# Three of four groups of W2 in seven block products with tokens down the partitions, and the branch weights' two parts made by transfers

## The chip, the cores and the metric

The kernel runs on one core of one Trainium2 chip. The time is the device time of one launch in microseconds (us); of several runs the median is given. TensorE (PE; PEld is its weight load), VectorE (DVE), ScalarE (ACT), GpSimd (POOL) and SyncE (SP, which only issues transfers) each have an instruction queue of their own that runs in order. Before, all transfers are issued from SP; the change issues some from POOL, which round to another type or add to what stands at the destination.

## The reference, cut to what matters

Two layers of an encoder on 512 tokens of 1024 channels. Each layer has a mixing half (projections, two kinds of softmax attention, a retention, three gated branches, an output projection) and an MLP. The change lies in the MLP's second matrix and in how the branch weights are prepared.

```python
projected = jnp.einsum('bsnw,nwd->bsnd', branches, w_branch[l])
gates = jax.nn.sigmoid(gate_logits.reshape(B, S, N_BRANCHES, D))
merged = jnp.sum(gates * projected, axis=2)
h = h + jnp.einsum('bsd,de->bse', merged, w_out[l])

m = jnp.einsum('bsd,df->bsf', rms_norm(h, mlp_norm[l]), w_mlp_in[l])     # W1: 1024 -> 4096
m = jnp.square(jax.nn.relu(m))
h = h + jnp.einsum('bsf,fd->bsd', m, w_mlp_out[l])                       # W2: 4096 -> 1024
```

## The kernel before, in words

All arithmetic is float32. The matmuls run on the type `F32R`; for it the kernel cuts every operand into a first part `hi` (ScalarE's copy rounds it) and a rest `lo` (VectorE subtracts), and each product is three matmuls: hi x hi, hi x lo, lo x hi (`passes`, line 568). Weights come in pieces ("quarters") of [128, 1024], 512 KB each: SP loads one into `stage`, ScalarE makes `w_hi`, VectorE makes `w_lo` (`cut_to`, line 512). The pool of such parts, `p_w`, holds six pairs.

Activations stand with channels down the partitions and tokens along the columns. W1 (`pair`, line 644) goes by pairs of 128 output columns in Winograd's form of Strassen's scheme: seven block products instead of eight, each of 12 matmuls with 256 columns, 84 in all. Its weights are cut by `cut_pair` (line 535), which takes three pairs of `p_w` (and one half pair of `p_wh`). The products run in the order 1, 2, 6, 5, 7, 4, 3; the first pair of parts serves 1 and 2, the second 6 and 5, the third 7 and 3.

W2 goes in four groups of 1024 hidden channels (`mlp`, line 1335). A group has eight units of 128 output channels; a unit is one sum in PSUM over eight tiles of hidden channels, three matmuls each with 512 columns: 24 matmuls (`prod_a`). The first group's sums are copied to SBUF (`mo`), the second and third are added to them, the third is multiplied by 1 / rms (`mo<-mo,rs`) and added to the stream `h`, the fourth goes from PSUM to `h`. `mlp_order` (line 52) weaves the four pairs of the next group's W1 into a group's W2: two within it, two behind it.

The merge at the end of the mixing half computes for each of three branches eight gate units and eight `proj` units; a branch has four quarters of weights (`("br", n, i)`), 12 a layer.

Every instruction is first noted and then put in an order (`Plan.order`, line 303): a simulated run in which each engine takes its first ready instruction, by the place where it was noted, with estimated durations (`price`, line 212) and the pools' free slots. The emitted program has that fixed order on each engine's queue, so an instruction whose input is late holds up what stands behind it.

Of the kernel before, what the change touches and what calls it, by code (L numbers as in the profile page):

```python
# [28 lines left out]
# positions of the small per-layer vectors in the row that every partition receives  # L29
# [14 lines left out]
GATE_PAIRS = {1: 8, 0: 2, 2: 0}  # L44
GATE_BANKS = ("mm", "sc", "tr")
# the gates after which the right operands of those pairs are made, four steps in all
TURN_AT = [(1, 4), (1, 6), (1, 6), (0, 0)]
# after which units of W2 the first pairs of the next group's W1 come
WOVEN = (3, 6)


def mlp_order():
    """W1 goes by pairs of units, W2 by units, in four groups of eight; a group's W1 starts within the W2 before it."""
    pairs = lambda g, k: [("w1", g, 2 * i) for i in k if g < 4]
    seq = pairs(0, range(4))
    for g in range(4):
        n = 0
        for i in range(8):
            while n < len(WOVEN) and WOVEN[n] == i:
                seq += pairs(g + 1, [n])  # L60
                n += 1
            seq.append(("w2", g, i))
        seq += pairs(g + 1, range(n, 4))
    return seq


def weight_plan():
    """Quarters of [128, 1024] in the order in which the core uses them: (key, matrix, rows, columns)."""
# [40 lines left out]
    for what, g, i in mlp_order():  # L109
        if what == "w1":  # L110
            for f in (g * 8 + i, g * 8 + i + 1):
                a_unit(("w1", f), "w_mlp_in", cols(f * 128, 128))
        else:
            a_unit(("w2", g, i), "w_mlp_out", cols(i * 128, 128), r0=g * 1024)
    return plan
# [5 lines left out]
# units whose weights are used two by two, in seven products instead of eight (Winograd's form of Strassen's)  # L121
PAIRED = {WIDX["w1", f] for f in range(0, 32, 2)} | {WIDX["gate", n, i] for n in GATE_PAIRS for i in range(GATE_PAIRS[n], 8, 2)}

BUFS_STAGE = 2
BUFS_W = 6
BUFS_WH = 2
BUFS_MID = 3
AHEAD_LOAD = 6
AHEAD_SPLIT = 2
# [27 lines left out]

class Ref:
    """A view of such a tile."""
# [82 lines left out]
class Op:  # L242
    __slots__ = ("engine", "name", "args", "kwargs", "key", "cost", "deps", "tiles", "new", "left", "outs", "end",
                 "ready")


class Plan:
    """Notes instructions as nc's engines are called, and issues them in the order of a simulated run."""
# [15 lines left out]
    def note(self, engine, name, args, kwargs):  # L264
# [30 lines left out]
        o.cost = price(engine, name, kwargs) if engine != "sync" else self.dma_price(kwargs)  # L295
        self.ops.append(o)
# [6 lines left out]
    def order(self):  # L303
        """A run in which every engine takes the first of its ready instructions, by key."""
# [7 lines left out]
        # slots: tiles of a tag in the order of their keys  # L312
# [11 lines left out]
        def ahead(g, pos):  # L324
            """Tiles before this one that have no slot yet."""
# [21 lines left out]
        while len(result) < n:  # L347
# [22 lines left out]
            for e in self.ENGINES:  # L370
# [27 lines left out]
                heapq.heappush(events, (now + o.cost + self.LATENCY.get(e, 0.0), 0, pick))  # L398
# [29 lines left out]
class Core:  # L428
    def __init__(self, ctx, tc, a):
# [3 lines left out]
        def pool(name, bufs, **k):  # L433
            return Pool(ctx.enter_context(tc.tile_pool(name=name, bufs=bufs, **k)), bufs, "space" in k)
# [6 lines left out]
        self.p_s = pool("s", 1)  # L441
# [17 lines left out]
        self.loaded = self.cut = 0  # L459
        self.stage, self.w = {}, {}  # L460
# [20 lines left out]
    # ---- weights: load and cut into two parts that TensorE's fast float32 takes exactly  # L481
    def load(self, n):
        while self.loaded < min(n, L * NQ):
            q = self.loaded
            t = self.p_stage.tile([128, 1024], F32, tag="stage", name="stage")
            self.nc.sync.dma_start(out=t, in_=self.a["w"][q])
            self.stage[q] = t
            self.loaded += 1

    def prefetch(self, i):  # L490
        n = min(i + AHEAD_SPLIT, L * NQ)
        while self.cut < n:
            self.load(self.cut + BUFS_STAGE)
            self.cut_to(self.cut + 1)
        self.load(min(i + AHEAD_LOAD, self.cut + BUFS_STAGE))

    def first_quarter(self, x):
        """The first quarter comes in pieces of 512 columns, each behind the tile of the stream that it meets."""
# [11 lines left out]
        self.loaded = self.cut = 1  # L510

    def cut_to(self, n):
        nc = self.nc
        while self.cut < n:
            q = self.cut
            if q % NQ in PAIRED:
                self.load(q + 2)
                self.w[q] = self.cut_pair(self.stage.pop(q), self.stage.pop(q + 1))
                self.cut += 2
                continue  # L520
            t = self.stage.pop(q)
            hi = self.p_w.tile([128, 1024], F32R, tag="hi", name="w_hi")
            lo = self.p_w.tile([128, 1024], F32R, tag="lo", name="w_lo")
            nc.scalar.copy(out=hi, in_=t)
            nc.vector.tensor_tensor(out=lo, in0=t, in1=hi, op=ALU.subtract)
            self.w[q] = (hi, lo)
            self.cut += 1

    def part(self, pool, n, t):
        hi = pool.tile([128, n], F32R, tag="hi", name="w_hi")  # L530
        lo = pool.tile([128, n], F32R, tag="lo", name="w_lo")
# [3 lines left out]
    def cut_pair(self, q0, q1):  # L535
        """Both parts of the seven left operands, each [128, 4 x 128]; q0 is [A11 | A12], q1 [A21 | A22]."""
        nc = self.nc
        lt, rt = slice(0, 512), slice(512, 1024)
# [15 lines left out]
    def weights(self, l, key):  # L554
        q = l * NQ + WIDX[key]
        self.prefetch(q + 1)
        return self.w[q]
# [18 lines left out]
    def head_rstd(self, ss, t, name):  # L576
        """1 / rms over a head of 64, for sums of squares that lack the token's own factor: its eps carries it."""
# [9 lines left out]
    # ---- RMSNorm: the products run on x g, and the tokens' 1 / rms scales what comes out of them  # L587
# [4 lines left out]
    def feed(self, x, k, which, u):  # L592
        """One [128 d, 512] tile of the stream: both parts of x g."""
# [4 lines left out]
    def feed_pair(self, x, j, which, u):  # L598
        """Tiles j and 4 + j of x g as right operands of the seven products: token halves B11, B12 and B21, B22."""
# [26 lines left out]
    def right(self, u, n, p, j):  # L626
        """Part p of the right operand of product n, k tile j: [128, 256 tok]."""
# [919 lines left out]
```

## Time and profile before

| what | value |
|---|---|
| median of 3 runs | 1793.13 us (1792.23 to 1793.45) |
| profiled execution, first to last instruction (span) | 1791.8 us |
| matmuls on TensorE | 10216 |
| TensorE clock granted | full in nearly every slice (1.00) |
| busy: PE, DVE, ACT, POOL | 99%, 77%, 55%, 17% of the span |
| moved by transfers | 172.50 MB, mean 96 GB/s |

The runs lie 0.4 to 1.7 us above the span of the profiled execution: that much lies around the first and last instruction. The first layer's stages in the profiled execution are: attention and projections to about 245 us, merge 245 to 517.6, output projection to 561.2, MLP to 898; the second layer repeats them.

### The profile page before, as it was taken

How to read it: one execution, taken by the hardware profiler on the slowest of the kernel's cores; microseconds unless marked ns; L12 is line 12 of the kernel's file. 1: busy time of each engine (PE TensorE's matmuls, PEld its weight loads, DVE VectorE, ACT ScalarE, POOL GpSimd, SP SyncE). 2: the span in 40 equal slices, each digit the busy share in tenths (PEclk: the TensorE clock that was granted, in tenths of full speed). 3: DMA queues.
4: the chain of work that ended last, by engine and by line, in shares of the span. 5: the costliest groups of instructions: out<-in, count | busy, mean ns of one | idle time of the engine just before them, and what ended most of it. 6: DMA issues, size and time to landing. Idle time of an engine off the chain costs nothing.

```text
span 1791.8 us, 26264 instructions
## 1 busy us (share of the span) xinstructions
PE 1767.7 (99%) x10216; PEld 1544.8 (86%) x10216; DVE 1376.4 (77%) x2084; ACT 983.2 (55%) x1568; POOL 297.1 (17%) x294
## 2 busy tenths in 40 slices
PE   8999999999999999999999999999999999999999
PEld 6887888889989989999888778888888899989897
DVE  7866797899979766678656677968999797566783
ACT  5545666784446655445444455768844466444450
POOL 3334472002210000000013335700111100000000
PEclk9999999999999999999999999999999999999999
DMA  6311212112352323333432121121133423234331
GB/s 203 105 61 49 93 49 79 59 37 95 107 170 101 118 94 118 123 115 116 152 106 71 48 80 62 59 63 56 39 104 130 159 83 134 95 102 128 121 113 56
DMA packets 53691, 172.50 MB, mean 96 GB/s; under 512 B 6336, under 2 KB 6848, under 8 KB 53568
## 3 DMA queue, kind: packets, MB, share of 16 engines
q1 hardware_dynamic: 53568, 170.84, 29.4%
q8 instruction: 80, 1.31, 0.3%
q14 instruction: 43, 0.35, 0.1%
HBM read 162.43 MB, written 8.39 MB: 95 GB/s over the span
## 4 chain that ended last, share of the span: by engine, by line
PE 82%; DVE 8%; issue 3%; POOL 3%; ACT 2%; DMA 1%; SPq 0%; DVEq 0%; ACTq 0%; POOLq 0%
PE x L411 21%; PE w L411 20%; PE gate L411 6%; PE proj L411 5%; PE wo L411 5%; PE c L411 4%; PE wtr L413 2%; PE rv L411 2%; DVE w_lo L417 2%; PE rg L411 2%; PE rq L411 2%; PE dsc L411 2%; PE gav L411 2%; PE gsc L411 2%; DVE c L417 1%
## 5 line engine op out<-in xcount | busy, mean ns | idle before, releaser
L417 ACT CAST w_hi<-stage 128x1024 fp32r<-128x1024 f32 (+1 forms) x283 | 276.6, 982 | 319.7 <-PE w L411 120.7
L417 DVE TENSOR_TENSOR w_lo<-stage,w_hi 128x1024 fp32r<-128x1024 f32 (+1 forms) x283 | 336.9, 1192 | 78.7 <-ACT w_hi L417 75.8
L411 PE MATMUL x<-u,w_hi 128*128 128x256 f32 x1472 | 273.5, 284 | 5.3 <-DVE c L417 5.3
L411 PEld LDWEIGHTS x<-u,w_hi 128*128 128x128 f32 x1472 | 232.3, 192 | 10.9 <-DVE c L417 8.2
L411 PE MATMUL x<-u,w_lo 128*128 128x256 f32 x736 | 208.0, 283 | 0.0
L411 PE MATMUL w<-ml,w_hi 128*128 128x512 f32 (+1 forms) x520 | 200.3, 386 | 0.0
L411 PE MATMUL w<-mh,w_lo 128*128 128x512 f32 (+1 forms) x520 | 200.1, 386 | 0.0
L411 PE MATMUL w<-mh,w_hi 128*128 128x512 f32 (+1 forms) x520 | 200.1, 387 | 0.0
L411 PEld LDWEIGHTS x<-u,w_lo 128*128 128x128 f32 x736 | 141.1, 192 | 0.0
L417 ACT ACTIVATE c<-c 128x512 f32<-128x512 f32 x156 | 98.4, 631 | 32.9 <-DVE c L417 30.2
L411 PEld LDWEIGHTS w<-mh,w_lo 128*128 128x128 f32 x520 | 97.8, 188 | 19.5
L411 PEld LDWEIGHTS w<-ml,w_hi 128*128 128x128 f32 x520 | 97.8, 188 | 18.7
L411 PEld LDWEIGHTS w<-mh,w_hi 128*128 128x128 f32 x520 | 97.8, 188 | 18.5
L411 PE MATMUL gate<-u,w_hi 128*128 128x512 f32 x320 | 107.3, 399 | 0.0
L411 PE MATMUL x<-t23h,w_lo 128*128 128x256 f32 x368 | 104.2, 283 | 0.0
L411 PE MATMUL x<-t23l,w_hi 128*128 128x256 f32 x368 | 104.0, 283 | 0.0
L411 PE MATMUL x<-t23h,w_hi 128*128 128x256 f32 x368 | 103.9, 283 | 0.0
L417 ACT CAST w_hi<-sa 128x1024 fp32r<-128x1024 f32 x46 | 48.5, 1053 | 77.0 <-DVE sa L417 55.9
L411 PE MATMUL c<-w_hi,u 128*128 128x512 f32 x256 | 86.1, 394 | 0.0
L417 POOL TENSOR_TENSOR gth<-gth,c 128x512 f32<-128x512 f32 x28 | 45.9, 1647 | 179.0 <-DVE c L417 179.0
L417 DVE TENSOR_TENSOR c<-x,pu 128x512 f32<-128x512 f32 x92 | 63.1, 686 | 12.0 <-PE x L411 11.3
L411 PEld LDWEIGHTS x<-t23l,w_hi 128*128 128x128 f32 x368 | 70.6, 192 | 0.0
(278 smaller groups left out, 4554.5 us busy)
## 6 DMA issues: line engine op xcount, KB each, us to landing
stage<-in_w SPq DMA_DIRECT2D x283, 512.0 KB, 3.6
h<-in_x SPq DMA_DIRECT2D x16, 256.0 KB, 5.3
mid<-h SPq DMA_DIRECT2D x16, 256.0 KB, 2.0
h<-mid SPq DMA_DIRECT2D x16, 256.0 KB, 4.8
keep<-h SPq DMA_DIRECT2D x8, 256.0 KB, 4.1
h<-keep SPq DMA_DIRECT2D x8, 256.0 KB, 3.9
out<-h SPq DMA_DIRECT2D x7, 256.0 KB, 2.0
t_ret<-in_t_ret SPq DMA_DIRECT2D x4, 256.0 KB, 4.9
```

The source lines that it names most:

```text
L411: self.nc.tensor.matmul(k.pop("out"), **k)
L413: self.nc.tensor.transpose(k["out"], k["in_"], k["identity"])
L417: getattr(getattr(self.nc, o.engine), o.name)(**k)
```

## The change

Three things are changed.

**W2's groups 0, 1 and 2** take the seven products too, with blocks of 512 hidden channels, 256 tokens and 512 output channels. The activations are now the operand that TensorE loads and the weights the one that moves, so sums come out with tokens down the partitions. A product is 2 sums of 12 matmuls with 512 columns (`wide_product`): 24 as in a unit, but seven a group. `rights` makes the seven blocks of the activations out of the group's eight tiles `c` and cuts each in parts (`xh`, `xl`). `cut_wide` makes the seven blocks of the weights: A11, A12 and A22 by `cut_dma`, the four combined ones on VectorE out of extra loads, the first of them (A21 + A22) by a transfer that adds. ScalarE copies every sum to `wp`; the first group's are stored in DRAM (`sums`), the next two groups' are added there by transfers from POOL. In group 3, which keeps its eight units, `gather` reads the 14 sums back, combines them, transposes them on TensorE (`turn`), multiplies them by 1 / rms and adds them to the stream.

**The branch weights**: `cut_dma` takes the place of `cut_to`'s cut. POOL issues a transfer that rounds DRAM's values to `hi`, ScalarE writes -hi to `lo`, POOL issues a transfer that adds the same DRAM values to `lo`. The VectorE subtraction goes; both weights are read twice.

**Pools and the planner**: `p_w` has five pairs instead of six, `sa` three buffers instead of one; weights are prepared two steps of a list `STEPS` ahead; `price` counts a matmul 11 ns longer, and POOL's transfers have estimates of their own.

```diff
-WOVEN = (3, 6)
+WIDE_GROUPS = (0, 1, 2)
+WOVEN = {True: (2, 4), False: (3, 6)}
...
+WIDE = ("A11", "A12", "A22", "S1", "S2", "S4", "S3")
+WIDE_PRODUCTS = (1, 2, 4, 5, 6, 3, 7)
...
-BUFS_W = 6
+BUFS_W = 5
-AHEAD_LOAD = 6
-AHEAD_SPLIT = 2
+AHEAD = 2
...
-            return 2.5 + n / 2.4 * (1 if n >= 256 else 4)
+            return 13.7 + n / 2.4 * (1 if n >= 256 else 4)
...
-        self.p_s = pool("s", 1)
+        self.p_s = pool("s", {"sa": 3, "sb": 1})
...
+    def cut_dma(self, q):
+        nc = self.nc
+        hi, lo = self.parts(self.p_w, 1024)
+        nc.gpsimd.dma_start(out=hi, in_=self.a["w"][q])
+        nc.scalar.activation(out=lo, in_=hi, func=AF.Copy, scale=-1.0)
+        nc.gpsimd.dma_start(out=lo, in_=self.a["w"][q], accum_op=ALU.add)
+        return hi, lo
...
+        def add(t, x):
+            nc.vector.tensor_tensor(out=t, in0=t, in1=self.load(at(x)), op=ALU.add)
+        if op == "A11":
+            w[k] = self.load(at("A21"), self.p_s, "sa")
+            nc.gpsimd.dma_start(out=w[k], in_=self.a["w"][at("A22")], accum_op=ALU.add)
+        if op[0] == "A":
+            return self.cut_dma(at(op))
+        if op == "S3":
+            w[k] = self.load(at("A21"))
+        if op != "S1":
+            add(w[k], {"S2": "A11", "S3": "A11", "S4": "A12"}[op])
+        return self.part(self.p_w, 1024, w[k])
...
-            if g == 0:
-                total[i] = self.g("mo")
-                nc.scalar.copy(out=total[i], in_=p)
-            elif g < 3:
-                nc.vector.tensor_tensor(out=total[i], in0=total[i], in1=p, op=ALU.add)
-                if g == 2:
-                    nc.vector.tensor_tensor(out=total[i], in0=total[i], in1=r2, op=ALU.mult)
-                    nc.vector.tensor_tensor(out=h[i], in0=h[i], in1=total[i], op=ALU.add)
...
+    def rights(self, m):
...
+        for n in WIDE_PRODUCTS:
+            if n == 4:
+                for j in range(4):
+                    b1, b2 = m[j], m[4 + j]
...
+                    sub(b1[:, rt], b2[:, rt], b1[:, rt])
+                    nc.vector.tensor_tensor(out=b1[:, lt], in0=b1[:, rt], in1=b1[:, lt], op=ALU.add)
+                    sub(b2[:, lt], b2[:, lt], b1[:, lt])
+                    sub(t1[-1][:, j % 2 * 256:j % 2 * 256 + 256], b2[:, rt], b1[:, lt])
...
+    def wide_product(self, l, g, o, x):
+        nc, n = self.nc, WIDE_PRODUCTS[o]
+        ps = [self.psum("mm", f"wide{n}") for _ in range(2)]
+        for k in range(2):
+            hi, lo = self.weights(l, ("w2", g, o), k)
+            xh, xl = x[k]
+            for s in range(2):
+                for j in range(2):
+                    t = slice(j * 256 + s * 128, j * 256 + s * 128 + 128)
+                    c = slice(j * 512, j * 512 + 512)
+                    self.passes(ps[s], [(xh[:, t], hi[:, c]), (xh[:, t], lo[:, c]), (xl[:, t], hi[:, c])],
+                                k == 0 and j == 0, k == 1 and j == 1)
+        for s, p in enumerate(ps):
+            y = self.g("wp")
+            nc.scalar.copy(out=y, in_=p)
+            if g == WIDE_GROUPS[0]:
+                nc.sync.dma_start(out=self.sums[n, s], in_=y)
...
+                nc.gpsimd.dma_start(out=self.sums[n, s], in_=y, accum_op=ALU.add)
```

TensorE, where the first group's W2 begins in the first layer. `w` is a W2 unit's sum before (`mh`, `ml` the parts of the hidden tiles), `x` a product of W1, `wide` a sum of the new products. Before:

```order
L411 MATMUL w_6498<-ml,w_hi 128x512
L411 MATMUL x_6444<-t4h,w_hi 128x256
L411 MATMUL x_6444<-t4l,w_hi 128x256
...
L411 MATMUL w_6498<-mh,w_lo 128x512
L411 MATMUL w_6498<-mh,w_hi 128x512
```

Now:

```order
L462 MATMUL x_6462<-t4h,w_lo 128x256
L462 MATMUL wide_6531<-w_hi,xh 128x512
L462 MATMUL wide_6531<-w_lo,xh 128x512
L462 MATMUL wide_6531<-w_hi,xl 128x512
L462 MATMUL wide_6568<-w_hi,xh 128x512
...
L462 MATMUL wide_6614<-w_hi,xh 128x512
L462 MATMUL wide_6628<-w_hi,xh 128x512
L462 MATMUL x_6651<-u_5703,w_hi 128x256
```

The matmuls have the same sizes; now the weights' parts are the moving operand, and two sums (6531 and 6568, then 6614 and 6628) grow side by side. The second matmul of a group already needs a `w_lo`.

POOL from the last gates of the first layer's merge to the MLP, the first group's weights and the first accumulations of `sums`. Before, POOL had nothing between the merge and the next layer:

```order
L417 TENSOR_TENSOR gth<-gth,c_5507 128x512
L417 TENSOR_TENSOR gth<-gth,c_5568 128x512
L417 TENSOR_SCALAR vmu<-vsum 128x4
L417 TENSOR_TENSOR rs<-ms,mhalf 128x4
```

Now, with the transfers that it issues (`sa` is A21 + A22, `w_hi` and `w_lo` the two parts):

```order
L468 DMA w_hi<-in_w 128x1024
L468 TENSOR_TENSOR gth<-gth,c_5337 128x512
L468 DMA w_lo<-in_w 128x1024
L468 TENSOR_TENSOR gth<-gth,c_5391 128x512
L468 TENSOR_TENSOR gth<-gth,c_5504 128x512
L468 TENSOR_TENSOR gth<-gth,c_5565 128x512
L468 DMA sa<-in_w 128x1024 x2
L468 DMA w_hi<-in_w 128x1024 x2
L468 DMA w_lo<-in_w 128x1024
...
L468 DMA w_lo<-in_w 128x1024 x3
L468 DMA sums_104<-wp 128x512
```

A branch's `w_lo` stands between the merge's additions, and a group's `w_hi` and `w_lo` stand one behind the other with the accumulations behind them; each `w_lo` waits for ScalarE, which waits for that `w_hi` to land.

ScalarE, around the start of the first group's W2. Before (`mo` is the copy of a unit's sum):

```order
L417 ACTIVATE c_6349<-c_6349 128x512 x2
L417 CAST mh<-c_6349 128x512
L417 ACTIVATE c_6420<-c_6420 128x512 x2
L417 CAST mh<-c_6420 128x512
L417 CAST w_hi<-stage 128x1024 x2
```

Now (`w_lo<-w_hi` is -hi, `xh` a first part of a block of the activations, `pu` a copy out of PSUM that W1 waits for):

```order
L468 ACTIVATE c_6352<-c_6352 128x512
L468 ACTIVATE w_lo<-w_hi 128x1024
L468 ACTIVATE c_6352<-c_6352 128x512
L468 COPY pu<-x_6360 128x256
L468 CAST xh<-c_6352 128x256
L468 ACTIVATE c_6419<-c_6419 128x512 x2
L468 ACTIVATE w_lo<-w_hi 128x1024
L468 CAST xh<-c_6419 128x256
```

A -hi, which waits for a transfer, now stands in ScalarE's queue ahead of the activations, the copies out of PSUM and the blocks' first parts.

Counted over the whole program, TensorE loses 1152 matmuls of W2 units and gains 1008 of wide products and 64 transposes. VectorE loses 60 `w_lo<-stage` of 1024 columns, 48 `ml`, 32 `mo<-mo,w`, 16 `mo<-mo,rs` and 16 `h<-h,mo`; it gains 36 `w_lo<-sa` and 36 additions of 1024 columns, 96 block sums and 144 `xl` of 256 columns, 12 `xl` of 512, 28 additions of `wp`, 16 `y<-turn` and 16 `h<-h,y`. ScalarE's 60 -hi take the place of 60 `w_hi`; it loses 48 `mh` and 16 `mo`, makes 36 `w_hi` more out of `sa`, and gains 144 `xh` of 256 and 12 of 512 columns and 84 `wp`. POOL issues 188 transfers: 60 that round to `hi`, 60 that add to `lo`, 12 that add to `sa`, 56 that add to `sums`. SP loses 24 loads of `stage` and gains 12 of `sa`, 28 stores of `sums` and 28 loads of `wp`.

## Rows read from the trace of the kernel before

**Rows 1.** The page: busy time by engine, and the last-ending chain.

```profile
PE 1767.7 (99%) x10216; PEld 1544.8 (86%) x10216; DVE 1376.4 (77%) x2084; ACT 983.2 (55%) x1568; POOL 297.1 (17%) x294
...
PE 82%; DVE 8%; issue 3%; POOL 3%; ACT 2%; DMA 1%; SPq 0%; DVEq 0%; ACTq 0%; POOLq 0%
```

**Rows 2.** Chain in the first MLP by line; pieces (start, us, what).

```profile
by line: PE w L411 51.7%; PE x L411 47.8%; PE ms L411 0.2%; PE rb L413 0.1%; PE wo L411 0.1%
...
517.60 43.60 PE wo L411 x192
...
619.18 8.63 PE x L411 x72
...
908.04 13.43 PE rv L411 x59
...
399.97 0.77 PE wtr L413 x7
```

**Rows 3.** Stretches: length; busy PE, PEld, DVE, ACT, POOL; clock, DMA share, GB/s.

```profile
245.00:410.00 165.00, 164.44 (x964) 142.11 (x963) 141.22 (x266) 125.38 (x247) 35.19 (x43) 1.00 0.18 60
410.00:517.60 107.60, 104.83 (x716) 96.76 (x715) 100.45 (x131) 46.59 (x62) 20.37 (x13) 1.00 0.40 133
604.65:688.15 83.50, 83.50 (x527) 75.97 (x527) 54.21 (x73) 44.23 (x62) 0.00 (x0) 1.00 0.32 103
688.15:772.10 83.95, 83.95 (x530) 76.34 (x529) 56.00 (x77) 39.05 (x53) 0.00 (x0) 1.00 0.36 117
772.10:856.10 84.00, 84.00 (x530) 76.39 (x529) 66.03 (x91) 40.02 (x54) 0.00 (x0) 1.00 0.39 132
856.10:898.30 42.20, 42.20 (x187) 34.93 (x187) 28.38 (x37) 18.40 (x26) 0.00 (x0) 1.00 0.48 140
```

**Rows 4.** Merge, 410 to 517.6: matmuls of proj, then x (windows).

```profile
410.00:517.60 107.60, 40.71 (x168) 1.00 0.40 133
...
410.00:517.60 107.60, 68.00 (x540) 1.00 0.40 133
```

**Rows 5.** The chain in the merge: start, us, what.

```profile
434.11 1.22 DVE w_lo L417
...
457.97 3.54 DMA stage<-in_w
```

**Rows 6.** DVE, 604.65 to 856.1: count | busy us, mean ns | idle before.

```profile
L417 DVE TENSOR_TENSOR w_lo<-stage,w_hi 128x1024 fp32r<-128x1024 f32 x38 | 46.5, 1224 | 29.4 <-ACT w_hi L417 29.4
...
L417 DVE TENSOR_TENSOR ml<-c,mh 128x512 fp32r<-128x512 f32 x24 | 16.5, 686 | 2.2 <-ACT mh L417 2.1
...
L417 DVE TENSOR_TENSOR w_lo<-sa,w_hi 128x1024 fp32r<-128x1024 f32 x12 | 14.6, 1217 | 0.8 <-ACT w_hi L417 0.8
L417 DVE TENSOR_TENSOR mo<-mo,w 128x512 f32<-128x512 f32 x16 | 11.0, 687 | 27.8 <-PE w L411 27.8
L417 DVE TENSOR_TENSOR c<-x,c 128x256 f32<-128x256 f32 x24 | 10.1, 420 | 0.8
```

**Rows 7.** ACT in the same stretch, same columns.

```profile
L417 ACT CAST w_hi<-stage 128x1024 fp32r<-128x1024 f32 x38 | 39.9, 1051 | 80.6 <-PE w L411 52.7 <-PE x L411 19.1 <-DMA stage<-in_w 8.8
...
L417 ACT CAST mh<-c 128x512 fp32r<-128x512 f32 x24 | 14.9, 622 | 0.8
...
L417 ACT COPY mo<-w 128x512 f32<-128x512 f32 x8 | 4.6, 579 | 0.0
L417 ACT COPY pu<-x 128x256 f32<-128x256 f32 x12 | 4.5, 373 | 2.9 <-PE x L411 2.5
```

**Rows 8.** DVE's weight cut, whole span; POOL, 245 to 517.6 (same columns).

```profile
L417 DVE TENSOR_TENSOR w_lo<-stage,w_hi 128x1024 fp32r<-128x1024 f32 x237 | 305.6, 1291 | 78.7 <-ACT w_hi L417 75.8 <-PE proj L411 0.7
...
L417 POOL TENSOR_TENSOR gth<-gth,c 128x512 f32<-128x512 f32 x13 | 20.4, 1573 | 88.9 <-DVE c L417 88.9
```

**Rows 9.** Transfers: KB each, us to landing; the densest 2 us (windows).

```profile
stage<-in_w SPq DMA_DIRECT2D x283, 512.0 KB, 3.6
...
20.00:22.00 2.00, 2.00 (x10) 1.65 (x9) 1.92 (x8) 0.20 (x1) 0.16 (x1) 1.00 1.04 423
```

More of the change, by code (lines that the diff above doesn't have):

```diff
@@ L56, in mlp_order @@
     for g in range(4):
-        n = 0
-        for i in range(8):
-            while n < len(WOVEN) and WOVEN[n] == i:
+        n, wide = 0, g in WIDE_GROUPS
+        for i in range(7 if wide else 8):
+            while n < 2 and WOVEN[wide][n] == i:
                 seq += pairs(g + 1, [n])
@@ L122, with steps @@
 PAIRED = {WIDX["w1", f] for f in range(0, 32, 2)} | {WIDX["gate", n, i] for n in GATE_PAIRS for i in range(GATE_PAIRS[n], 8, 2)}
+WIDE = ("A11", "A12", "A22", "S1", "S2", "S4", "S3")
+WIDE_PRODUCTS = (1, 2, 4, 5, 6, 3, 7)
+def steps():
+    out, at = [], {}
+    q = 0
+    while PLAN[q][0][0] != "w1":
+        at[PLAN[q][0]] = len(out)
+        out.append(("pair" if q in PAIRED else "dma" if PLAN[q][0][0] in BY_DMA else "one", q))
+        q += 2 if q in PAIRED else 1
+    for what, g, i in mlp_order():
+        at[(what, g * 8 + i) if what == "w1" else (what, g, i)] = len(out)
+        if what == "w1":
+            out.append(("pair", WIDX["w1", g * 8 + i]))
+        elif g in WIDE_GROUPS:
+            out += [("wide", WIDX["w2", g, 1, 1, 0], WIDE[i], k) for k in range(2)]
+        else:
+            out.append(("one", WIDX["w2", g, i]))
+    return out, at
+STEPS, STEP_AT = steps()
+NS = len(STEPS)
 BUFS_STAGE = 2
-BUFS_W = 6
+BUFS_W = 5
 BUFS_WH = 2
 BUFS_MID = 3
-AHEAD_LOAD = 6
-AHEAD_SPLIT = 2
+AHEAD = 2
 BUFS_G = 51
@@ L242 @@
 class Op:
-    __slots__ = ("engine", "name", "args", "kwargs", "key", "cost", "deps", "tiles", "new", "left", "outs", "end",
-                 "ready")
+    __slots__ = ("engine", "name", "args", "kwargs", "key", "cost", "late", "deps", "tiles", "new", "left", "outs",
+                 "end", "ready")
 class Plan:
@@ L295, in note @@
         o.cost = price(engine, name, kwargs) if engine != "sync" else self.dma_price(kwargs)
+        o.late = self.LATENCY.get(engine, 0.0)
+        if engine == "gpsimd" and name == "dma_start":
+            o.cost, o.late = (880.0, 5600.0) if "accum_op" in kwargs else (600.0, 3800.0)
         self.ops.append(o)
@@ L397, in order @@
                 result.append(pick)
-                heapq.heappush(events, (now + o.cost + self.LATENCY.get(e, 0.0), 0, pick))
+                heapq.heappush(events, (now + o.cost + o.late, 0, pick))
                 heapq.heappush(events, (busy[e], 2, pick))
@@ L458, in __init__ @@
         nc.sync.dma_start(out=self.gains, in_=a["gains"])
-        self.loaded = self.cut = 0
-        self.stage, self.w = {}, {}
+        self.cut = 0
+        self.w, self.wide = {}, {}
     def tables(self):
@@ new lines, in mlp @@
+                    m.append((self.g("mh", F32R), self.g("ml", F32R)))
+                    self.split(c, *m[-1])
+                continue
+            if g in WIDE_GROUPS:
+                if i == 0:
+                    rights = self.rights(m)
+                    nxt = next(rights)
+                now, nxt = nxt, next(rights, None)
+                self.wide_product(l, g, i, now)
+                continue
+            if i == 0:
+                gather = self.gather(h, mid, load, r2)
+            if i in GATHERED:
+                next(gather)
@@ L1435, in trunk @@
             tiles.append(k.ref())
+    core.sums = {}
+    for n in WIDE_PRODUCTS:
+        for s in range(2):
+            k = Tile(None, [128, 512], F32, None, "sums")
+            k.real = p_dram.tile([128, 512], F32, name=f"sums{n}{s}")
+            core.sums[n, s] = k.ref()
     def load(src, i):
```

166 lines of the change are left out of this document (109 added, 57 removed).

## The prediction

> **What bounds the kernel now.** I read the page first: PE is busy 99% of the span and holds 82% of the chain that ended last, DVE 8% [rows 1]. So a change is worth what it takes off TensorE, if nothing else then ends later. A busy PE is not yet a PE at its pace, so next I read the chain of the MLP: W2's matmuls (`w`) and W1's (`x`) are 99.5% of it, and its long pieces give the paces: 192 matmuls of 512 columns in 43.60 us, 0.2271 us each; 72 of 256 columns in 8.63 us, 0.1199 each; transposes 0.77 / 7 = 0.110 [rows 2]. A cycle of W2 and the next group's W1 is 192 x 0.2271 + 336 x 0.1199 = 83.9 us, and the stretches 688.15 to 772.10 and 772.10 to 856.10 last 83.95 and 84.00 [rows 3]: in the MLP nothing but TensorE's pace counts. DVE there is busy 54 to 66 us of each, the transfers' share is 0.32 to 0.39.
>
> The merge differs. In 410 to 517.6 DVE is busy 100.45 of 107.6 us, 93% [rows 3], and DVE's work and loads stand on the chain [rows 5]. TensorE has 168 `proj` and 540 `x` matmuls there [rows 4]: 168 x 0.2271 + 540 x 0.1199, and 7 of an attention sum, is 103.7 us. So 93% of DVE went with 3.9 us lost, 3.7%.
>
> **W2 on TensorE.** 1152 matmuls go, 1008 come, all of 512 columns. That the weights now move changes no pace: `rv` already does so, 59 in 13.43 us, 0.2276 each [rows 2]. The gain is 144 x 0.2271 = 32.7 us. The 64 transposes cost 64 x 0.110 = 7.0 us. They lie on TensorE, which has no idle time to hide them. Net -25.7 us.
>
> **DVE in the MLP.** A wide group adds 40 operations of 256 columns at 0.42 (16.8 us), two of 512 (1.4), six additions of 1024 columns and eight `w_lo` at 1.22 (17.1): 35.3 us. No addition of 1024 columns has a row; the subtraction of that size is the nearest. Every cycle loses eight `w_lo` (9.8) and, of 512 columns, eight operations in the first (`ml`; 5.5), 16 in the second (`ml`, `mo`; 11.0) and 24 in the third (16.5) [rows 6]. The cycles go from 54.2, 56.0 and 66.0 us to 74.2, 70.5 and 75.0 [rows 3], in 168 x 0.2271 + 336 x 0.1199 = 78.4 us: 95%, 90%, 96%. Group 3 adds 14 `wp`, 8 `y` and 8 `h`, 30 x 0.687 = 20.6 us, to its 28.4 in 42.2 us; TensorE needs 43.6 + 3.5 = 47 there, so some of it must run under the W1 pairs ahead. The lower end is nothing lost, since 66 of 84 us cost nothing. The upper end is the merge's rate, 3.7% of 6 x 78.4 us = 17.4. I take 5: four of the six cycles are at the merge's load, but their work is less chained to single products than the gates' is.
>
> **ACT in the MLP** gains, per group, 24 blocks at 0.373, 2 at 0.62, 14 copies at 0.579 and six more passes over 1024 columns at 1.05, and loses eight `mh` at 0.622 [rows 7]: about 20 us, so some 60 of 78.4. Enough room: nothing for its work, but it runs in order, and a -hi that waits for a transfer holds up the copies out of PSUM.
>
> **The weights made by transfers.** A11, A12 and A22 need: POOL's issue, a transfer that rounds, -hi on ACT, POOL's issue, a transfer that adds, then the matmul. For how much time there is, follow the five pairs of `p_w`. Of the W1 pair ahead of a group the first pair of parts is free after two of its seven products, the second after four, the third at its end; a pair lasts 84 x 0.1199 = 10.07 us, a wide product 5.45, half of it for the first k. So the first product's second half gets its buffer 10.07 us before the product and is needed 2.7 us into it: 12.8. The second product's halves get 7.2 + 5.45 = 12.6 and 4.3 + 8.2 = 12.5 us; A22's, freed by the second product and needed behind a pair, 12.8. How long does it take? The rounding transfer has no row; a plain load of the same bytes lands in 3.6 us [rows 9], and I take that, up to 4.4 with a busier queue. -hi: 1.05 [rows 7]. The transfer that adds lies between 3.6 (like a load) and 7.2 (twice the bytes read). POOL's issue has no row either: between nothing and the 1.57 us of a POOL addition [rows 8], twice; hand-overs I put at 0.5 in all. Sum: 8.8 to 16.3 us, middle 12.5, against 12.6. The transfers are thus just in time: lateness 0 to 3.7 us at two places in each of six groups, 0 to 44 us. At the middle they are late only when the queue is full; I take 0.4 at each of the 12 places, 5 us.
>
> Here a page speaks against the change. By the rows, a cycle's 16 loads each occupy the DMA engines for 0.32 x 83.5 / 16 = 1.67 us, or 512 KB at 423 GB/s = 1.24 us when they are packed [rows 3, 9]. The Trainium skill's "Collectives: The Full Stack" (The bandwidth ceiling: the fold count and why AG ≠ RS ≠ AR) says that an add in a transfer reads two sources through one ring and so moves at half a copy's rate. No row here shows a transfer that adds. By that rule the add takes the upper of the two values above and the time goes to the first rival's, 1791 or more; by the rows alone it is like a load, and the sum below holds.
>
> **The sums through DRAM.** 84 stores or additions of 256 KB and 28 loads; they end long before `gather`: the last product of group 2 lies two W1 pairs (20 us) and three units (16 us) before its sums are needed, the first five one product earlier. Nothing. If that cover failed, the transposes would hold TensorE by the excess.
>
> **The branch weights.** 24 `w_lo` of 1.29 us leave DVE, 31 us [rows 8], ACT's work stays. In the merge at most the 3.9 us a layer come back, 7.8; at least nothing, since loads are on that chain too. I take half, -4. POOL gets 48 transfers there; a `w_lo` waits for two steps, and behind it stand the `gth` additions. POOL is busy 55.6 of 272.6 us [rows 3], so this is hidden; if not, a few us at the merge's end.
>
> **The planner** now counts a matmul at nearly the measured 0.2271 us (13.7 ns + 512 / 2.4), which also reorders the attention; either sign, I count nothing.
>
> **Sum.** 1791.8 (span) - 25.7 + 5 + 5 - 4 = 1772.1. The runs lie 0.4 to 1.7 us above that execution's span, their median 1.3: **1773 us**.
>
> **Rivals.** *Transfers late at the group starts (slower).* Per group 24 pieces are loaded where eight were, eight of them added, and up to 14 sums are added too. If an add takes its engines twice as long, then in the 24 us around a group's start (four roundings and adds, two `sa`, three or four loads, two sums) there are about 4 x 3.9 + 2 x 3.9 + 5.2 = 28.6 us of work at 1.3 us each: it does not fit, and the chain above is at its upper end. 12 x 3.7 = 44 us instead of 5: 1812; if only the group's start is late, 22 us: 1791. For it: 24 against eight loads, and a sum that is just in time. Against it: the mean share today is only 0.32 to 0.39. It decides (slower than before) from (1793 - 1768) / 12, about 2.1 us late at each place: with 4 us for the rounding and 0.8 for each issue, an add that lands after 14.7 - 4 - 1.05 - 1.6 - 0.5 = 7.5 us.
>
> *DVE becomes the bound.* At 95% in four cycles and above 100% for group 3 unless its sums move forward, the loss is 17.4 in the cycles and about 4 at the two ends: 1793.1 - 25.7 - 4 + 21 + 5 = 1789. For it: the merge at 93%; against it: the cycle from 772 to 856, with 79%, loses nothing, and its work waits on PE as that of the new cycles would.
>
> *All hidden.* Adds land like loads, DVE never late, and the merge gives back 6 us: 1793.1 - 25.7 - 6 = 1761. For it: the MLP's clean pace today.
>
> **How the numbers follow.** Forecast (1766 to 1784) 0.52; all hidden 0.20; DVE-bound 0.14; transfers late 0.14. A difference under 0.2% (3.6 us) can't be told from none here. Faster: the first two and half of the third, 0.79; same: most of the third's rest and the mild end of the last, 0.08; slower: what is left, 0.13. The range 1760 to 1794 leaves out the strong form of late transfers and better than all hidden.
>
> **What would show it.** The profile after should have `wide` at 0.227 us a matmul, cycles of 78.4 to 80 us for wide groups, and idle PE, if any, at the first two products and at A22, released by a transfer of `w_lo`. In the merge DVE's share should fall below 90% with PE's loss under 3.9 us. Wrong: cycles above 82 us; adds that land after 7.5 us; DVE pieces on the MLP's chain; or the attention longer through POOL's waits, which I price at nothing.

## The result: 5% slower, and the profile after

The changed kernel takes 1885.9 us (median of 4 runs, 1884.4 to 1888.6) beside 1793.1 us (4 runs): 92.8 us more, ratio 1.052, interval 1.051 to 1.054. The forecast was 1773 us, in a range of 1760 to 1794.

The page after: busy time by engine, the chain by engine and by line, and transfers (KB each, median us to landing).

```profile
PE 1784.2 (95%) x10136; PEld 1538.5 (82%) x10136; DVE 1436.1 (76%) x2296; ACT 1074.3 (57%) x1780; POOL 444.8 (24%) x482
...
PE 46%; DMA 16%; DVE 15%; issue 9%; POOL 7%; ACT 6%; SPq 0%; POOLq 0%; DVEq 0%; ACTq 0%
...
w_hi<-in_w POOLq DMA_DIRECT2D x60, 512.0 KB, 4.5
w_lo<-in_w POOLq DMA_DIRECT2D x60, 512.0 KB, 7.0
```

Beside [rows 1], TensorE's share of the chain fell from 82% to 46%; transfers have 16% and DVE 15%. The rounding transfer (`w_hi`) and the adding one (`w_lo`), which had no row, land in 4.5 and 7.0 us (medians over the whole run).

Stretches of the changed kernel, columns as in [rows 3]: the three wide cycles of layer 1, each from the end of one group's W1 to the end of the next one's.

```profile
621.09:717.18 96.09, 83.36 (x507) 72.96 (x506) 66.88 (x103) 58.33 (x94) 11.22 (x15) 0.98 0.80 225
717.18:810.74 93.56, 85.13 (x506) 76.52 (x505) 67.72 (x110) 55.82 (x90) 22.80 (x29) 0.93 0.90 219
810.74:902.38 91.64, 83.42 (x511) 74.62 (x510) 71.23 (x108) 54.77 (x86) 15.45 (x19) 0.97 0.84 226
```

In [rows 3] PE was busy for the whole of each cycle and the transfers' share was 0.32 to 0.39. Now the share is 0.80 to 0.90, and PE is idle for 12.7, 8.4 and 8.2 us. The forecast had 78.4 to 80 us for a cycle, and said "wrong" from 82.

What TensorE stands for in this MLP (waiting group, what ended the wait, us in all, times, longest); then the chain over the three cycles, its shares and some of its pieces; then what the two kinds of queue carried there (packets, MB, share of 16 engines) and plain loads (KB, us to landing).

```profile
PE wide L462 <- DMA w_lo<-in_w: 9.0, 4, 3.9
PE x L462 <- DVE w_lo L468: 6.3, 4, 3.0
PE x L462 <- DVE c L468: 6.2, 6, 2.2
PE x L462 <- ACT w_hi L468: 4.8, 3, 2.3
```

```profile
by line: DMA stage<-in_w 27.6%; issue 12.6%; PE wide L462 10.7%; PE x L462 8.2%; DMA w_lo<-in_w 7.1%; DVE w_lo L468 6.1%; DVE sa L468 4.4%; DVE xl L468 4.2%; ACT w_hi L468 3.6%; DMA w_hi<-in_w 3.0%; DVE stage L468 2.2%; DMA sa<-in_w 2.1%; D
...
756.28 5.37 DMA stage<-in_w
761.74 1.24 DVE stage L468
...
765.41 5.54 DMA stage<-in_w
771.04 1.24 DVE stage L468
...
774.63 7.04 DMA stage<-in_w
```

```profile
q0 software_dynamic: 9069, 25.65, 46.5%
q1 hardware_dynamic: 12383, 36.91, 37.7%
...
stage<-in_w SPq DMA_DIRECT2D x50, 512.0 KB, 5.3
```

The reader should see four things. The blocks' late rest parts, the only wait for transfers that the forecast priced, are 9 us of the waits in the list; W1's products (`x`), which the change does not touch, have 17. The largest line of the chain is the plain load, 5.3 us now in place of 3.6 [rows 9]. POOL's queue (`q0`), with 70% of the other one's bytes, takes more of the DMA engines. And idle time is not the whole loss: the three cycles are 46 us longer than three of 78.4, of which PE is idle for 29; in the rest it counts as busy, but is slower (last section).

### The profile page after: what moved, and what is told of

It reads as the page before. It is cut to its first block, busy times and chain, and to the rows that moved or that the text cites. A ratio compares the mean times of both kernels' runs of the same rounds, so it can differ in the third digit from the quotient of the medians.

```text
span 1884.6 us, 27015 instructions
## 1 busy us (share of the span) xinstructions
PE 1784.2 (95%) x10136; PEld 1538.5 (82%) x10136; DVE 1436.1 (76%) x2296; ACT 1074.3 (57%) x1780; POOL 444.8 (24%) x482
## 3 DMA queue, kind: packets, MB, share of 16 engines
q0 software_dynamic: 27072, 83.90, 21.7%
## 4 chain that ended last, share of the span: by engine, by line
PE 46%; DMA 16%; DVE 15%; issue 9%; POOL 7%; ACT 6%; SPq 0%; POOLq 0%; DVEq 0%; ACTq 0%
DMA stage<-in_w 11%; PE x L462 7%; PE proj L462 5%; PE wo L462 5%; PE w L462 5%; PE gate L462 4%; DVE w_lo L468 4%; PE wide L462 3%; DMA w_lo<-in_w 2%; ACT w_hi L468 2%; PE c L462 2%; DVE sa L468 2%; PE wtr L464 2%; PE rq L462 2%; DMA w_hi<-in_w 2%
## 5 line engine op out<-in xcount | busy, mean ns | idle before, releaser
L468 ACT CAST w_hi<-stage 128x1024 fp32r<-128x1024 f32 (+1 forms) x223 | 213.9, 962 | 282.8 <-DMA stage<-in_w 108.9
L468 DVE TENSOR_TENSOR w_lo<-stage,w_hi 128x1024 fp32r<-128x1024 f32 (+1 forms) x223 | 262.0, 1176 | 68.7 <-ACT w_hi L468 64.2
L462 PE MATMUL wide<-w_lo,xh 128*128 128x512 f32 x336 | 135.4, 403 | 21.8 <-DMA w_lo<-in_w 21.7
L462 PE MATMUL wide<-w_hi,xl 128*128 128x512 f32 x336 | 132.9, 397 | 0.0
L462 PE MATMUL wide<-w_hi,xh 128*128 128x512 f32 x336 | 128.7, 397 | 3.4 <-ACT wp L468 2.0
L468 DVE TENSOR_TENSOR w_lo<-sa,w_hi 128x1024 fp32r<-128x1024 f32 x82 | 100.2, 1222 | 22.3 <-ACT w_hi L468 21.8
L462 PEld LDWEIGHTS wide<-w_lo,xh 128*128 128x128 f32 x336 | 64.5, 192 | 39.4 <-DMA w_lo<-in_w 27.0
L468 POOL DMA_DIRECT2D w_lo<-in_w x60 | 52.9, 881 | 165.2 <-ACT w_lo L468 130.2
L468 POOL DMA_DIRECT2D sums<-wp x56 | 49.0, 890 | 162.5 <-ACT wp L468 111.0
L468 ACT ACTIVATE w_lo<-w_hi 128x1024 fp32r<-128x1024 f32 x60 | 63.4, 1057 | 36.5 <-DMA w_hi<-in_w 35.0
```

The source lines that it names most:

```text
L462: self.nc.tensor.matmul(k.pop("out"), **k)
L468: getattr(getattr(self.nc, o.engine), o.name)(**k)
```

## The experiments

Three questions: which part costs what (E1, E2, E3, E6, E11, E17), what limits W2's form with transfers (E7, E8, E9, E12, E13, E14), and what limits it without them (E4, E10, E15, E16, E18, E19). "Before" in the same sessions ran in 1791.8 to 1793.1 us. The two runs of E1 are 14 us apart, 1860.9 and 1874.5, so a difference to E1 of less than some 10 us shows nothing.

### Which part costs what

**E1**, branch weights on the engines again:

```diff
-BY_DMA = {"br"}
+BY_DMA = set()
```

> The branch weights are loaded and cut on ScalarE and VectorE again; W2 keeps its seven products with blocks by transfers. My theory (a rounding and an adding transfer fill the DMA engines, so that loads and parts come late; the merge loses about 16 us in each layer to it and the MLP about 30): 1886 - 2 x 16 = 1854 us, with wo beginning at about 518 us in layer 1. Rival (the new planner prices and the smaller weight pool cost the time before wo): 1886 us still, wo at 534.

**E2**, `WIDE_GROUPS = ()`, with W2's units and totals written as before:

> W2 goes by units of eight products as before; only the branch weights come by transfers (with the new planner prices and pools). My theory: 1793 + 2 x 16 = 1825 us. Rival (the branch weights by transfers are harmless, and what goes before wo is lost comes from what the W2 transfers of the layer leave behind): 1793 us or a little less.

**E3**, both edits:

> W2 by units and the branch weights cut on the engines; what stays of the change is the planner's price of a product, five buffers for weights, steps looked ahead in another way, and three sa tiles. My theory: 1793 us within 4. Rival (planner and pools): 1810 us or more, most of it in the merge.

Measured: E1 1867.7, E2 1822.5, E3 1810.1 us. E1 lies between its two cases, with `wo` at 526.9 us and not at 518. My theory fell for E3: 17 us are lost with neither of the two parts in. So E2 came near my 1825 by luck, since 17 of its 30 us are in E3 too. Against E3 the branch weights' transfers cost 12.3 us and W2's new form 57.6 (51 to 64 by E1's two runs). The weight pools and the planner's price, from E3's rival, were then tried apart. **E6** gives E3 its sixth weight buffer back:

```diff
-BUFS_W = 5
+BUFS_W = 6
...
-        self.p_s = pool("s", {"sa": 3, "sb": 1})
+        self.p_s = pool("s", {"sa": 1, "sb": 1})
```

> The kernel with neither part of the change (1810 us) gets its sixth buffer for weights back, in place of two of the three sa tiles. Theory pool (units of four quarters hold four of the five buffers, so that only one further quarter is cut ahead): 1793 us within 3, wo of layer 1 at 517 to 518 us. Rival (the planner's price of a product, 13.7 ns more, or the looking ahead by steps): 1808 us still.

**E11** is the kernel before with one number of `price` changed:

```diff
-            return 2.5 + n / 2.4 * (1 if n >= 256 else 4)
+            return 13.7 + n / 2.4 * (1 if n >= 256 else 4)
```

> The kernel before with one number changed: the planner's price of a product is 13.7 ns more than its columns give, as in the changed kernel, in place of 2.5. Theory price (it is what the kernel with neither part still lost, 17 us, all of it ahead of wo): 1805 to 1812 us, wo of layer 1 at 525 to 527 us. Rival (the looking ahead by steps, with which loads follow the cuts): 1793 us.

E6: 1809.5, nothing back. E11: 1808.8 us, ratio 1.009 (1.006 to 1.012): the price alone is worth 16.7 us. It changes no work, only the order. In the trace of E11, a stretch of the attention (columns as in [rows 3]) and `wo` on the chain:

```profile
245.00:410.00 165.00, 162.11 (x912) 135.89 (x911) 136.68 (x260) 122.77 (x241) 35.27 (x44) 1.00 0.18 60
...
525.50 43.60 PE wo L411 x192
```

Before, the same 165 us held 964 matmuls [rows 3] and `wo` began at 517.60 [rows 2]. Up to `wo` TensorE has the same matmuls in both, 2787 and 2786 by the windows; of the 7.9 us more, 5.6 count as busy and 2.3 as idle, so the idle time alone doesn't show the loss. Which step of the attention stands worse in the new order was not tested.

**E17** gives the changed kernel the old price, the same line the other way.

> The changed kernel as it is (1886 us) with the planner's old price of a product. Theory (the price costs 16 us in the mixing whatever the rest does): 1870 us within 4. Rival (price and the rest share their losses): 1880 us or more.

1874.5 us: 11.4 less, between the two cases. In its trace the two mixing halves (from a layer's start to its `wo`) are 18 us shorter than in the changed kernel, as the theory had it, but from `wo` to the MLP's end the two layers are 6 us longer: the price's loss is not a separate sum. Nor is the price all that costs the mixing. With the old price the mixing halves of E15, E18 and E19 are still 10, 16 and 10 us longer than before; E3 with the old price, which would tell whether pools and looking ahead do that, was not run.

For the branch weights, the merge of layer 1 in E3 (first) and in E2, columns as in [rows 3], and what POOL waits for in E2:

```profile
410.00:526.00 116.00, 112.31 (x772) 103.29 (x771) 103.57 (x142) 51.48 (x74) 22.63 (x14) 1.00 0.35 119
```

```profile
410.00:526.00 116.00, 112.04 (x775) 103.12 (x774) 93.96 (x135) 52.33 (x75) 31.00 (x26) 1.00 0.54 146
...
POOL w_hi L468 <- PE x L462: 39.9, 6, 11.9
POOL w_lo L468 <- ACT w_lo L468: 22.1, 4, 7.1
```

DVE does fall, from 89% to 81% of the stretch, and PE is busy no longer. In place of DVE, POOL's queue stands up to 11.9 us for a weight buffer and 7.1 us for -hi, with the `gth` additions behind. That the 12 us go there was not tried by itself, and this merge holds little of them: in the traces `wo` begins 2.6 us later in E2 than in E3 in layer 1, and the mixing half of layer 2 is 7.7 us longer.

### What limits the form with transfers

All on E1 (1868 us). **E9** takes 7/8 of the bytes of the blocks' adding transfers away (so it leaves out most of the rest parts).

```diff
-        nc.gpsimd.dma_start(out=lo, in_=self.a["w"][q], accum_op=ALU.add)
+        nc.gpsimd.dma_start(out=lo[:, 0:128], in_=self.a["w"][q][:, 0:128], accum_op=ALU.add)
```

> The same kernel (1868 us), but the adding transfer that finishes a block's rest part fetches 128 of the 1024 columns only, so that the rest part is left as minus the first part elsewhere; the chain of round, negate, add and its queue stay, 16.5 MB of adding transfers go away. Theory traffic (adding transfers of the weights fill the DMA engines and make the loads late): loads land in under 4.5 us in the MLP again and 25 us or more come back: 1843 us or less. Rival stage or order: 1855 us or more, the waits for the rest part alone gone (about 10 us).

**E7** has a third stage buffer:

```diff
-BUFS_STAGE = 2
+BUFS_STAGE = 3
...
-BUFS_G = 51
+BUFS_G = 49
```

> W2 in seven products, branch weights cut on the engines (1868 us), with a third stage buffer and two fewer of the 128x512 tiles. Theory stage (two stage buffers with loads that take 5 to 7 us in place of 3.6 can't feed W1's cut; W1's products lost 23 to 25 us in each layer to late operands): at least half of it back, 1868 - 25 = 1843 us or less. Rival order (W1's parts are late because work on VectorE stands in the queue behind transfers that the planner believed to be faster): 1860 to 1868 us. Rival tiles (the 128x512 tiles are short): slower than 1868 us.

**E14** has both edits.

> W2 in seven products with blocks by transfers, branch weights on the engines, adding transfers for the rest part of 128 of 1024 columns only (rest part left as minus the first part elsewhere), and a third stage buffer. The thin adds alone gave 1856 us, the third buffer alone 1872, against 1868. Theory both (the third buffer helps only where the DMA engines have room): 1835 us or less. Rival queue (the blocks' round, negate and add stand in order on POOL and ScalarE, whatever the traffic): 1850 us or more.

Measured: E9 1856.1, E7 1872.2, E14 1841.0 us. The thin adds alone give 12 us (5 to 18 by E1's two runs), which is what E9's rival had: loads land in under 4.5 us again, yet the theory's 25 us don't come back. The buffer alone gives nothing that E1's spread lets one see, both together give 27. E14 misses the theory's 1835 by 6 and lies 9 under the queue rival's 1850. Between 610 and 850 us the DMA engines stand so in E7 (its queues, and loads) and in E9:

```profile
q0 software_dynamic: 8426, 24.88, 52.1%
q1 hardware_dynamic: 8909, 28.72, 35.2%
...
stage<-in_w SPq DMA_DIRECT2D x43, 512.0 KB, 5.3
```

```profile
q0 software_dynamic: 8263, 16.85, 36.2%
q1 hardware_dynamic: 9072, 28.77, 36.2%
...
stage<-in_w SPq DMA_DIRECT2D x42, 512.0 KB, 4.3
```

In E7 the queues hold 87% of the DMA engines, with loads at 5.3 us, and the third buffer gives nothing; in E9 72% with loads at 4.3 us, and then a third buffer is worth 15 us (E14). So the thin adds and the buffer are wanted together. That it is the room on the DMA engines is argued, not shown: the thin adds also shorten the blocks' own chain (an add lands in 3.2 us in E14, in 6.9 in E7), and no run takes the two apart. In E7 the late weight parts of W1 are no longer among TensorE's waits in layer 1's MLP, but the sums `c` that DVE returns late are:

```profile
PE x L462 <- DVE c L468: 12.4, 6, 3.9
```

The first two cycles of E14 (the third takes 93.38 us):

```profile
612.31:698.19 85.88, 81.18 (x508) 73.46 (x507) 67.39 (x109) 54.65 (x91) 10.46 (x14) 0.98 0.69 207
698.19:784.59 86.40, 80.31 (x506) 71.60 (x505) 67.23 (x108) 53.57 (x88) 21.88 (x27) 1.00 0.82 206
```

**E13** stores the products of groups 1 and 2 in place of adding them:

```diff
-            if g == WIDE_GROUPS[0]:
+            if True:
```

> The same kernel (1868 us), but the products of groups 1 and 2 are stored plainly by SP over those of the group before, not added, so that the output lacks the sums of groups 0 and 1. Takes away 56 adding transfers of 256 KB and their issue on POOL, 0.9 us each; as many plain stores come. Theory sums (they stand on POOL's queue, which the blocks' transfers share, and fill the DMA engines): 1868 - 25 = 1843 us or less. Rival: they are hidden, 1862 to 1868 us.

1861.2 us: 6.5 less than E1 and between its two runs, at the rival's edge. The theory's 25 us aren't there; whether the adding of the sums costs anything can't be told. **E8** plans with longer transfers:

```diff
-    LATENCY = {"sync": 2000.0}
+    LATENCY = {"sync": 5000.0}
...
-            o.cost, o.late = (880.0, 5600.0) if "accum_op" in kwargs else (600.0, 3800.0)
+            o.cost, o.late = (880.0, 8000.0) if "accum_op" in kwargs else (600.0, 6000.0)
```

> The same kernel (1868 us), but the planner takes 5.0 us in place of 2.0 for a plain load's latency and 6.0 and 8.0 us in place of 3.8 and 5.6 for the rounding and the adding transfer, about what they took in the MLP; the work is the same, only the order changes. Theory order: W1's products lose less, 1868 - 20 = 1848 us or less. Rival stage or traffic (the loads themselves set the pace): 1860 to 1875 us.

1890.4 us, slower than either case foresaw: an order that counts on later landings doesn't help. **E12** has six weight buffers:

```diff
-BUFS_W = 5
+BUFS_W = 6
...
-BUFS_G = 51
+BUFS_G = 47
```

> W2 in seven products, branch weights on the engines (1868 us), with six buffers for weights in place of five and 47 of the 128x512 tiles in place of 51. Theory pool (a block that comes by transfers holds its buffer from the first issue, some 14 us longer than one cut on the engines, so that W1's cut finds none): 1835 to 1850 us. Rival (W1's parts are late for loads or for VectorE's queue): 1862 to 1872 us.

1886.2 us. The pool theory is not borne out, but four 128x512 tiles went too, and which of the two edits costs some 18 us can't be told from this run.

### What limits the form on the engines

**E4** makes the blocks from plain loads:

```diff
-            nc.gpsimd.dma_start(out=w[k], in_=self.a["w"][at("A22")], accum_op=ALU.add)
+            add(w[k], "A22")
...
-            return self.cut_dma(at(op))
+            return self.cut_one(at(op))
```

> W2 in seven products and the branch weights by transfers, but the blocks A11, A12, A22 and the sum A21 + A22 are loaded plainly and made on ScalarE and VectorE; the sums of products still go through memory with adding transfers. My theory (the adding transfers of the weights fill the DMA engines in the MLP): the 28 to 33 us that a layer's MLP lost come back and some of the saved products show: 1805 to 1830 us. Rival 1 (VectorE becomes the bound: 36 subtractions of 1.3 us more in each layer's MLP): about 1870 to 1886. Rival 2 (the adding transfers of the sums or the order of products is what costs): 1875 to 1886.

1895.1 us: with the adds gone nothing comes back, outside all three cases. (Rival 1's 36 subtractions are 18 in each layer, 36 in all.) By the code the plain loads rise from 16 to 24 a cycle, with two buffers for them. **E10** adds E1's and E7's edits.

> W2 in seven products, everything cut on the engines (no transfer that rounds, only the sums are still added by transfers), and three stage buffers (two fewer 128x512 tiles). With two stage buffers and the branch weights by transfers this stood at 1895 us with 24 loads in a group's W2 and W1. Theory stage (there the two buffers were the limit, as each load holds one for 3.9 us and until the engines are done with it): 1835 to 1860 us. Rival VectorE (82 to 89 percent busy in those stretches, its queue in order): 1870 us or more.

1844.0 us, inside the theory's range and 51 us under E4. Some 18 of the 51 may be the branch weights', as from the changed kernel to E1; the rest fits E14, where a third buffer helped too. What is left in E10, its first two cycles and TensorE's waits in the MLP of layer 1:

```profile
615.18:699.08 83.90, 80.41 (x505) 73.02 (x504) 75.04 (x118) 54.91 (x91) 0.00 (x0) 0.98 0.64 208
699.08:789.40 90.32, 81.40 (x507) 73.31 (x506) 77.00 (x117) 55.80 (x92) 12.37 (x14) 0.98 0.70 192
...
PE x L462 <- DVE c L468: 20.3, 10, 4.9
```

PE waits for DVE alone, which adds the sums of products (`c`) that free the PSUM tiles; DVE is busy 85 to 89%. **E15** is E10 with the old price.

> Seven products with everything cut on the engines and three stage buffers (1844 us), with the planner's old price of a product. Theory price adds up: 1844 - 16 = 1828 us, the stretch ahead of wo shorter and the MLP as before. Rival (in the MLP the true price plans VectorE's queue better): 1840 us or more.

1813.9 us, 30 less where 16 were expected: some 20 of it in the two MLPs, where layer 1's first two cycles fall from 83.90 and 90.32 to 81.29 and 84.31 us (its third does not: 89.70 and 90.78). So an order that suits this form matters too. **E16** moves the blocks' subtractions to POOL:

```diff
-            return self.cut_one(at(op))
+            t = self.load(at(op))
+            hi, lo = self.parts(self.p_w, 1024)
+            nc.scalar.copy(out=hi, in_=t)
+            nc.gpsimd.tensor_tensor(out=lo, in0=t, in1=hi, op=ALU.subtract)
+            return hi, lo
```

> As e15, but the rest parts of A11, A12 and A22 are subtracted by POOL, which has little to do in the MLP, in place of VectorE: 36 instructions of 1.2 us less on VectorE. Theory VectorE (88 percent busy, PE waits for its sums of products alone): 10 to 25 us less than e15, 1803 to 1818 us. Rival (the waits come from the order, or from POOL's own queue, where the sums' transfers stand): within 5 us of e15 or slower.

1870.4 us, the rival. One subtraction holds POOL 3.5 us, and its queue waits (in E16's MLP of layer 1; POOL's group first, then its wait):

```profile
L468 POOL TENSOR_TENSOR w_lo<-stage,w_hi 128x1024 fp32r<-128x1024 f32 x18 | 63.7, 3546 | 164.1 <-ACT w_hi L468 111.2 <-PE x L462 53.0
...
POOL sums L468 <- ACT wp L468: 72.9, 15, 13.4
```

So E16 swapped one late engine for another and told nothing of DVE. **E18** relieves DVE without POOL (E15's kernel; it leaves out 7/8 of these rest parts):

```diff
...
+            nc.scalar.copy(out=lo[:, 128:1024], in_=t[:, 128:1024])
+            nc.vector.tensor_tensor(out=lo[:, 0:128], in0=t[:, 0:128], in1=hi[:, 0:128], op=ALU.subtract)
```

> As e15 (1814 us: everything cut on the engines, three stage buffers, old price), but VectorE subtracts 128 of the 1024 columns only of the rest parts of A11, A12 and A22, and ScalarE fills the others with the weights themselves (so these rest parts are not the rest): 36 instructions shorter by about 1 us each on VectorE, 36 of about 1 us more on ScalarE. Theory VectorE: 1795 to 1804 us. Rival (loads and ScalarE's queue are what is left): 1810 us or more.

1799.1 us, within the theory's 1795 to 1804. The first two cycles of E18:

```profile
612.32:690.37 78.05, 78.05 (x503) 71.45 (x503) 69.13 (x113) 59.06 (x95) 0.00 (x0) 1.00 0.64 218
690.37:770.85 80.48, 79.49 (x505) 72.04 (x505) 69.16 (x113) 58.68 (x96) 12.39 (x14) 1.00 0.76 216
```

The first is the cycle that the forecast had, 78.4 us; the third takes 89.54, of which 4.19 are matmuls of group 3 and 4.6 idle. From `wo` to the MLP's end the two layers of E18 together are 8 us shorter than before, and its mixing halves 16 us longer. So the saved products do save time once DVE's work and the weights' transfers are out of the way, less than the forecast's 15.7 us net. DVE's share is still 86 to 89% here, so the share by itself does not say whether TensorE waits. **E19** has `A21 + A22` by an adding transfer again:

> As e15, but A21 + A22 is made by an adding transfer as in the change: 12 loads and 12 additions of 1.2 us fewer in all for VectorE and the stage buffers, 12 adding transfers of 512 KB more. Theory VectorE: 1806 to 1812 us. Rival traffic (adding transfers cost more than they spare): 1816 us or more.

1810.5 us, 3.3 less than E15, inside the theory's range but near what one pair of runs can tell. It is the fastest kernel with wide groups that leaves nothing out, still at ratio 1.010 (1.007 to 1.013) to before. No run here beat the kernel before.

## Why the prediction was wrong, step by step

**The accounts.** My sum had -32.7 + 7.0 + 5 + 5 = -15.7 us for W2, -4 for the branch weights and nothing for the planner. By E3, E2 and E1 they are +57.6, +12.3 and about +17; together 87 of the 92.8 us. The missing 6 are within E1's spread.

**"The weights made by transfers ... 5 us": the step that failed most.** I followed the chain of one wide block, weighed 8.8 to 16.3 us against 12.6, and charged its lateness to the wide products alone. Both landings came out above my bounds (in the cycles, rounding 5.8 us, where I took up to 4.4; adding 7.7, where I had 3.6 to 7.2). The 0.5 us for hand-overs stood on no row; in the chain above DVE takes up a landing after 0.09 us. TensorE's waits for the blocks came where I said, at A11, A12 and A22, and are 22 us in the whole run, over my 5 and inside my 0 to 44:

```profile
PE wide L462 <- DMA w_lo<-in_w: 21.7, 13, 3.9
```

What failed is that I held fixed everything else on the same DMA engines. Their share rose from a third to 0.80 to 0.90, plain loads went from 3.6 to 5.3 us, and W1's cut, which works from two stage buffers, became late: in layer 1's MLP TensorE stands 11 us for W1's weight parts and 6 for its sums, beside 9 for the blocks. E14 shows that thin adds and a third buffer together give 27 us back; how much of that is W1's is open. The rival "Transfers late at the group starts" had the sign and the trigger (adds that land after 7.5 us; in the cycles 7.7), but its 44 us counted only the wide products' waits too.

**"DVE in the MLP ... I take 5."** I read DVE's load as a share, 90 to 96%, and priced it by the merge's loss at a like share. The share came out lower in the changed kernel, 70 to 78%: busy for 66.9 to 71.2 us where I had 70.5 to 75.0, in longer cycles, in which DVE itself waits for loads and for ScalarE's first parts, which wait for loads too:

```profile
ACT w_hi L468 <- DMA stage<-in_w: 30.0, 16, 4.2
DVE w_lo L468 <- ACT w_hi L468: 28.8, 25, 4.9
...
DVE sa L468 <- DMA stage<-in_w: 22.6, 12, 3.5
```

Where the loads are relieved, DVE is next: E10 to E18. On the engines E18's shorter subtractions, 29 us of DVE's busy time in all, took 15 us off. E18 against E15 is thus the nearest measure of that term in a form that isn't held up by transfers.

**"The branch weights ... -4"** had the wrong sign. DVE was relieved as forecast (below 90%), but the cost was written off with "this is hidden; if not, a few us": POOL waits 39.9 us for weight buffers in that stretch of E2. That this wait makes the 12.3 us is not shown.

**"The planner ... I count nothing"** was worth 17 us: E11 has no other edit.

**What held.** The paces: 168 matmuls of 512 columns and 336 of 256 at those of [rows 2] are the 78.4 us, and E18's first cycle takes 78.05. The sums through DRAM, "nothing": E13 shows no cost of adding them beyond E1's spread. The Trainium skill's "Collectives: The Full Stack" (The bandwidth ceiling: the fold count and why AG ≠ RS ≠ AR) has the adding transfers of a ReduceScatter at half a copy's rate, and I left that out of the sum. The landings are 5.4 us against 3.9 for a rounding transfer and 3.6 for a load in E2, so not double; in engine time it is nearer (below).

**What stays open.** Why the price of a product moves the mixing by 16 us; where E2's 12 us go in detail; why E18's `wo` still begins 8 us late, at 525.98 us, with the old price; how much of E14's 27 us is room for W1's loads and how much the blocks' shorter chain; and why six buffers and 47 tiles (E12) cost 18 us.

## What to carry to other kernels

When work moves to transfers, redo the account of everybody else's transfers on those engines: a stage that was clean at a third of their time need not be at nine tenths, and the first to be late may be a part that the change doesn't touch. A saving on the bound engine counts only if the helper engines keep time, and a busy share doesn't tell whether they do; who is waited for does. A change of a planner's constant is a change of its own: measure it alone.

## What the runs showed of the hardware

Rounding and adding transfers together took more of the DMA engines than plain loads of the same bytes. Queues in E2 (whole span; only the branch weights by transfers, half of the bytes rounded and half added):

```profile
q1 hardware_dynamic: 50112, 158.26, 26.7%
q0 software_dynamic: 6912, 25.17, 6.4%
...
w_hi<-in_w POOLq DMA_DIRECT2D x24, 512.0 KB, 3.9
w_lo<-in_w POOLq DMA_DIRECT2D x24, 512.0 KB, 5.4
```

A megabyte takes 0.169% of the span on the loads' queue and 0.254% on POOL's. If a rounding transfer costs what a load does (an assumption), the adding one takes 2.0 times as much. Each issue holds POOL too: 587 ns for a rounding transfer in the changed kernel, 881 for an adding one of the weights.

TensorE's granted clock, 1.00 in every MLP stretch of [rows 3], falls to 0.93 to 0.98 in the cycles after. Two short windows of the changed kernel:

```profile
706.00:712.00 6.00, 3.45 (x28) 3.14 (x27) 4.01 (x9) 2.27 (x4) 1.42 (x2) 1.00 1.10 323
712.00:717.00 5.00, 3.68 (x15) 3.40 (x16) 3.23 (x7) 4.94 (x9) 0.86 (x2) 0.66 1.06 263
```

The engine was idle 2.55 of 6 us at the upper level, 2.4 GHz, and then ran at a mean of 0.66 for 5 us, a mix of it and 1.2 GHz. The 336 `x` matmuls of a cycle, alone, before (first) and in the changed kernel (the second cycle of each; length, PE, PEld, DVE, ACT):

```profile
688.15:772.10 83.95, 41.24 (x337) 41.11 (x336) 10.55 (x20) 1.50 (x4) 1.00 0.36 117
```

```profile
717.18:810.74 93.56, 46.79 (x337) 45.29 (x336) 10.43 (x20) 1.50 (x4) 0.93 0.90 219
```

They count as busy for 5.5 us more here, and for 2.3 and 3.1 us more in the other two cycles. So waits came with slower work, and cost more than their own length; how much of this is the clock's was not measured apart.
